# Two units ahead of the FFN's norm, norm factors with positions on partitions, shorter routing, unread products in waits, and plain loads of the down tiles

## Chip, cores and metric

The kernel runs on one core of one Trainium2 chip. The metric is the time of one execution in device microseconds (us). A trace of one profiled execution tells what each engine did; its times count from the first instruction of the span.

## What is computed

A trunk of two layers over one sequence of 256 positions with 1024 features, all in float32. Each layer has a mixer and a channel mixer (FFN), each behind an RMS norm that is shifted and scaled by a conditioning vector. The FFN of layer 0 is dense; that of layer 1 sends each position to 2 of 8 experts.

```python
for l in range(DEPTH):
    mod = cond @ w_ada[l] + b_ada[l]
    sh_m, sc_m, gt_m, sh_f, sc_f, gt_f = jnp.split(mod[:, None, :], 6, axis=-1)
    h = _rmsnorm(x, g_norm_mix[l]) * (1 + sc_m) + sh_m
    x = x + gt_m * _hybrid_mixer(h, ...)
    h = _rmsnorm(x, g_norm_ffn[l]) * (1 + sc_f) + sh_f
    y = _swiglu(h, ...) if l % 2 == 0 else _moe(h, ...)     # d_ff 2816
    x = x + gt_f * y
return _rmsnorm(x, g_final)
# _swiglu: (silu(h @ w_gate) * (h @ w_up)) @ w_down
# _moe: logits = h @ w_router + b_router; top 2 of 8; softmax over the two; sum of gate_e * _swiglu_e(h)
```

## The kernel before, in words

**Data.** x is kept as xT, eight tiles k of 128 features by 256 positions. Weights come from HBM through SP's DMA queue, as "units" of at most 1 MB each (256 columns or 256 rows of a matrix), in the order in which they are used, into a ring of buffers; a unit is loaded as soon as a buffer is free (`fill`). Outside the experts a product of two float32 matrices is made as three fp32r products (L654 to L656): each operand is cut into a high part (a cast, ScalarE, "hi") and a rest (a subtraction, VectorE, "lo") by `split`, 1.9 and 2.2 us for a unit of 1024 x 256. A unit of 256 output columns then takes 8 k x 2 x 3 = 48 products of 256 columns. Units without a key are those of the ada matrix (`ada_unit`); VectorE alone works on them, and `ada_tail` or `ada_wide` turn their sums into columns of M.

**Stages.** Mixer 0 (to about 163 us), dense FFN (to about 358), mixer 1 (to about 495), experts (to about 1203), final norm. `row_product` makes the last product of a mixer or FFN, adds it into xT tile by tile (two j at a time) and, in `done`, squares each new tile for the sums of the norm that follows.

**Norms** (`rms_mod`, L772). While the last xT tiles are finished, `scaled_parts` cuts A*xT, not yet normalised, into "xa" (high and rest). The first unit of the next stage is multiplied with xa: L792 to L794, 48 products into two PSUM banks. Between them stand, at k = SUMK = 2, the last sums of squares over partitions (L861) and a copy of the sums ("rows"), and at k = ACROSS = 4 a product with ones (L786) that puts the sum on all partitions, 128x256; `nrstd` turns it into the factor rs_ (square root on ScalarE, reciprocal and one Newton step on VectorE, all 128x256). Then the eight tiles are normalised (ht) and cut (hh on ScalarE, hl on VectorE), and the next unit can be multiplied (`feat_major`, L654 to L656). `start(c, dst)` multiplies the products made ahead by rs_ and returns a bias. In the dense FFN the unit made ahead is ("gate", 0) and the first behind the norm ("up", 0); in mixer 1 it is ("xl", 1, 0).

**End of mixer 1.** `route_sums` takes for each j two products with the router's matrix (L1227), two transposes of xT into PSUM banks "ps_xt" (L1229) and, through `sums_small`, products of the squares with ones (L301). `ada_wide` makes the columns of ada group (1, 5), wanted only at the kernel's end: eight products (L416), a copy, a transpose (L418), an addition into M.

**Routing** (`moe`, from L1232). y is the norm's factor for each position, lg the logits, sel the two chosen experts of each position. Products L1268 to L1272 (bank "ps_pos") count places; posp is the place of a position in its expert's list, and `oh` the one-hot matrix of it. `normalised` makes xnh and xnl (high part and rest of the normalised rows with positions on partitions) from the transposes. `gather(0)` multiplies them with oh (L1443) into xf, the 96 rows of expert place 0; later gathers do so for the other sets.

**Experts.** Eight places, each of the kind M (CAP 96 rows) or S (64 rows): KINDS = "MSMMSMMS". Each goes over d_ff in groups of 1024, 1024 and 768 columns: four gate tiles and four up tiles (L1462 for S, L1469 for M, plain fp32), then `act` and, one group later, `turn` (transposes of the activations, L1499, L1502 and L1385) and `down` (L1539 for M, L1557 for S). The weights stay whole (`whole`), and each buffer is free when PE has used it. For kind M the last group of 768 rows of the down matrix is laid out so that two tiles are strided reads of 128 partitions, and the third consists of two transfers of 512 KB to 64 partitions each (L325, the list path of `load`).

**Order.** An automatic scheduler orders the instructions on each engine; ScalarE's and VectorE's instructions behind a `hold()` are not put ahead of it. `limit` and state["limit"] say up to which unit splits may run ahead; `next_unit` does the next one.

## Time and profile before

| | us |
|---|---|
| three runs, median | 1223.89 |
| lowest and highest | 1220.61, 1226.54 |
| the profiled execution's own time | 1221.15 |
| its span, first to last instruction | 1219.4 |
| PE busy | 1158.0 |
| VectorE busy | 517.6 |
| ScalarE busy | 308.2 |
| mean granted clock of PE (1 is full) | 0.981 |

In the rows, PE is TensorE's products and PEld its weight loads, DVE is VectorE, ACT ScalarE, SP the engine that issues the loads. A name like "ps_z<-hh,hi" says what is written and what is read. A timeline row gives start, duration, engine, line, operation, the count of merged instructions, and in brackets how long the engine was idle before and what released it. L112 is the line of a helper through which all ScalarE and VectorE instructions pass. Instructions on PE overlap: the time from one start to the next is shorter than the duration.

### The profile page before, as it was taken

To read this page: it belongs to the slowest core of one execution; us is meant where nothing else is said; L and a number is where in the kernel's file an instruction comes from. 1 tells how busy PE (TensorE), PEld (TensorE's weight loads), DVE (VectorE), ACT (ScalarE), POOL (GpSimd) and SP (SyncE) were. 2 spreads that over 40 slices of the span, in tenths; PEclk is the share of its full clock that TensorE was granted. 3 is DMA by queue.
4 is the path that set the end of the run, shared out by engine and by line. 5 is a ranking of instruction groups with operands and counts; after the bars stand their busy time and mean duration, and the time that the engine had idled before them with its cause. 6 is when DMAs were issued, how large, how long until landed. Compare 5 with 4: busy or idle time off the path is not lost.

```text
span 1219.4 us, 28948 instructions
## 1 busy us (share of the span) xinstructions
PE 1158.0 (95%) x12777; PEld 853.2 (70%) x12777; DVE 517.6 (42%) x947; ACT 308.2 (25%) x528; POOL 18.2 (1%) x49
## 2 busy tenths in 40 slices
PE   3899989999998999899999999999999999999994
PEld 3798879999997998666644667767545576666531
DVE  6799989988768985410110111020010111010123
ACT  3493465344346834200100001000000000000111
POOL 4000000000010000000000000000000000000000
PEclk9899999999999999799999999999999999999998
DMA  9976739989862856889999999999999999999991
GB/s 321 351 263 221 273 142 360 356 318 345 281 213 72 281 179 245 342 300 405 357 412 416 411 408 377 370 404 369 379 409 414 413 410 325 403 400 334 404 396 63
DMA packets 144419, 400.66 MB, mean 329 GB/s; under 512 B 6968, under 2 KB 50288, under 8 KB 144288
## 3 DMA queue, kind: packets, MB, share of 16 engines
q1 hardware_dynamic: 143296, 397.44, 87.5%
q8 instruction: 102, 1.67, 0.5%
q0 software_dynamic: 560, 1.16, 0.4%
q10 hardware_dynamic: 432, 0.15, 0.1%
q14 instruction: 29, 0.24, 0.1%
HBM read 397.67 MB, written 1.05 MB: 327 GB/s over the span
## 4 chain that ended last, share of the span: by engine, by line
PE 87%; DVE 8%; ACT 2%; issue 1%; DMA 1%; ACTq 0%; SPq 0%; DVEq 0%
PE ps_y L1539 12%; PE ps_g L1469 8%; PE ps_u L1469 8%; PE ps_gu L1469 8%; PE ps_z L656 5%; PE ps_z L654 5%; PE ps_z L655 5%; PE ps_g L1462 5%; PE ps_u L1462 5%; PE ps_y L1557 5%; PE ps_acc L654 2%; PE ps_acc L656 2%; PE ps_acc L655 2%; PE ps_acc L829 2%; PE ps_xg L1443 2%; DVE lo L112 2%
## 5 line engine op out<-in xcount | busy, mean ns | idle before, releaser
L654 PE MATMUL ps_z<-hh,hi 128*128 128x256 f32 x624 | 177.3, 285 | 4.6 <-ACT hh L112 3.9
L656 PE MATMUL ps_z<-hh,lo 128*128 128x256 f32 x624 | 175.8, 284 | 2.0 <-DVE lo L112 2.0
L655 PE MATMUL ps_z<-hl,hi 128*128 128x256 f32 x624 | 176.7, 284 | 0.1
L1469 PE MATMUL ps_gu<-raw,xf 128*32 128x256 f32 (+1 forms) x1920 | 151.1, 365 | 2.9 <-issue 2.9
L1539 PE MATMUL ps_y<-raw,aT 128*32 128x256 f32 (+1 forms) x1980 | 150.0, 451 | 0.0
L112 DVE TENSOR_TENSOR lo<-raw,hi 128x2048 fp32r<-128x2048 f32 x60 | 136.5, 2284 | 17.7 <-ACT sg L112 9.2
L1539 PEld LDWEIGHTS ps_y<-raw,aT 128*32 128x32 f32 x1980 | 93.0, 110 | 51.4 <-issue 2.4
L112 ACT CAST hi<-raw 128x2048 fp32r<-128x2048 f32 x59 | 111.8, 1905 | 56.5 <-PE ps_acc L655 26.5
L1469 PE MATMUL ps_g<-raw,xf 128*32 128x256 f32 (+1 forms) x1920 | 125.5, 367 | 0.0
L654 PEld LDWEIGHTS ps_z<-hh,hi 128*128 128x128 f32 x624 | 119.4, 192 | 5.7 <-ACT hh L112 4.1
L112 DVE SCALAR_TENSOR_TENSOR a<-a,gs,ps_u 128x256 f32<-128x256 f32 (+3 forms) x39 | 18.7, 512 | 246.3 <-PE ps_u L1469 118.9
L1469 PE MATMUL ps_u<-raw,xf 128*32 128x256 f32 (+1 forms) x1920 | 121.1, 364 | 0.2 <-issue 0.2
L656 PEld LDWEIGHTS ps_z<-hh,lo 128*128 128x128 f32 x624 | 118.6, 191 | 2.3 <-DVE lo L112 2.3
L655 PEld LDWEIGHTS ps_z<-hl,hi 128*128 128x128 f32 x624 | 119.5, 192 | 0.4 <-DVE hl L112 0.3
L112 DVE SCALAR_TENSOR_TENSOR acc<-raw,cond,acc 128x1024 f32<-128x1024 f32 x77 | 98.4, 1278 | 4.1 <-DMA raw<-in_w_ada_dram 3.2
L1469 PEld LDWEIGHTS ps_gu<-raw,xf 128*32 128x32 f32 x1920 | 71.1, 111 | 32.2 <-issue 4.9
L1469 PEld LDWEIGHTS ps_g<-raw,xf 128*32 128x32 f32 x1920 | 66.9, 111 | 33.3 <-issue 6.8
L1469 PEld LDWEIGHTS ps_u<-raw,xf 128*32 128x32 f32 x1920 | 68.6, 111 | 28.0 <-issue 2.4
L112 ACT COPY aT<-ps_t 128x512 f32<-128x512 f32 (+1 forms) x24 | 13.2, 550 | 257.6 <-PE ps_t L1514 164.5
L112 DVE COPY aT<-ps_t 128x256 f32<-128x256 f32 (+1 forms) x20 | 7.8, 390 | 143.2 <-PE ps_t L1514 73.1
L1462 PE MATMUL ps_g<-raw,xf 128*64 128x512 f32 (+1 forms) x288 | 61.8, 563 | 0.0
L1462 PE MATMUL ps_u<-raw,xf 128*64 128x512 f32 (+1 forms) x288 | 59.6, 559 | 0.0
(485 smaller groups left out, 1498.7 us busy)
## 6 DMA issues: line engine op xcount, KB each, us to landing
raw<-in_w_exp_down_dram SPq DMA_DIRECT2D x83, 1024.0 KB, 17.5
raw<-in_w_exp_gate_dram SPq DMA_DIRECT2D x64, 1024.0 KB, 17.6
raw<-in_w_exp_up_dram SPq DMA_DIRECT2D x64, 1024.0 KB, 17.9
raw<-in_w_ada_dram SPq DMA_DIRECT2D x40, 1024.0 KB, 5.8
raw<-in_w_in_dram SPq DMA_DIRECT2D x24, 1024.0 KB, 6.6
raw<-in_w_exp_gate_dram SPq DMA_DIRECT2D x32, 768.0 KB, 16.4
raw<-in_w_exp_up_dram SPq DMA_DIRECT2D x32, 768.0 KB, 14.8
raw<-in_w_ff_gate_dram SPq DMA_DIRECT2D x11, 1024.0 KB, 7.5
```

What stands on the lines that cost most here:

```text
L112: r = op(*a, **kw)
L654: TE.matmul(ps, wh, xh, start=first, stop=False, **kw)
L655: TE.matmul(ps, wh, xl, start=False, stop=False, **kw)
L656: TE.matmul(ps, wl, xh, start=False, stop=last, **kw)
L829: TE.matmul(out_, w[:, c, js], parts[c], start=start, stop=stop, skip_group_check=True)
L1443: TE.matmul(p, src[:, t, k * P:(k + 1) * P], oh[:, t, :w], start=n == 0 and t == 0, stop=n == 1 and t == 1)
L1462: TE.matmul(ps[0][b * 64:b * 64 + 64, :h], xf[:, k, :], w[:, q, b * h:(b + 1) * h], start=k == 0, stop=k == KD - 1)
L1469: TE.matmul(o[j * 32:j * 32 + 32], xf[:, k, g * 32:g * 32 + 32], w[:, q, j * h:(j + 1) * h], start=k == 0 and (g == 0 or g == 2 and key == ...
L1539: TE.matmul(y[bank_][r:r + 32, c:c + nd], x(g), w[:, b, d0:d0 + nd], start=first and start, stop=last, skip_group_check=True)
L1557: TE.matmul(y[0][h2 * 64:h2 * 64 + 64], ah[:, o + b * 64:o + b * 64 + 64], w[:, c, ns], start=first, stop=last)
```

## The change

1. `rms_mod` takes a list of units. The dense FFN multiplies gate 0 and up 0 with xa ahead of the norm; mixer 1 still one unit. The sums stand at step 2, the factor at step 4, its spread over the partitions at step 7, counted over both units. The factor is made with positions on partitions (128x2): two products with a column of ones, `nrstd` on 128x2, then `all_across` (two diagonal matrices, two fp32 products) and a ScalarE copy to rs_. The next unit's split (gate 1) stands ahead of the normalisation.
2. `route_sums` no longer uses sums of squares by products; ScalarE squares the transposed banks with a running sum (four instructions of 128x512), and `done` makes no squares there.
3. `ada_wide` is cut in two: the eight products and the bias stay, copy, transpose and addition move to expert 0.
4. In `moe`, four ScalarE copies make the normalised rows xn (float32); the first gather uses xn and oh as fp32; xnh and xnl are made in expert 0's second group.
5. `warm(n)` issues n products of 128x512 (fp32r, ones by ones) that nobody reads: 12 behind the ada products, 3 behind the place products, 6 behind mixer 1's products ahead of the norm.
6. The last down tiles of kind M are plain loads of 256 rows; `turn` makes the matching layout with three banks and three more transposes, `down` picks its columns accordingly.
7. ss0 and nw0, at the kernel's beginning, lie in another pool.

```diff
+WARM = 12, 3, 6
+SUMS_AT, FACTOR_AT, ACROSS_AT = 2, 4, 7
...
     def load(ap, shape, pool=rawp, tag="raw"):
-        if isinstance(ap, list):
-            v = raw[:, :shape[0] * shape[1]].rearrange("p (a b) -> p a b", a=shape[0])
-            for i, x in enumerate(ap):
-                nc.sync.dma_start(v[i * 64:(i + 1) * 64], x)
-            return v
...
     def ada_wide(l, g):
+        acc, ps = accs.pop((l, g)), bank("ps_ada")
         for j in range(KD):
             TE.matmul(ps[:KD, :P], pick[:, j, :], acc[:, j * P:(j + 1) * P], start=j == 0, stop=j == KD - 1)
-        S.copy(am, ps[:KD, :P])
-        TE.transpose(ps[:, P:P + KD], am, ident[:KD, :KD])
-        V.tensor_add(M[l][:, g * KD:(g + 1) * KD], ps[:, P:P + KD], colr("b_ada", l * 48 + g * KD, KD, C1))
-        known.add((l, g))
+        m = M[l][:, g * KD:(g + 1) * KD]
+        V.tensor_copy(m, colr("b_ada", l * 48 + g * KD, KD, C1))
+
+        def turned(pool):
+            am = pool.tile([P, P], F32, name="am")[:KD]
+            S.copy(am, ps[:KD, :P])
+            TE.transpose(ps[:, P:P + KD], am, ident[:KD, :KD])
+            V.tensor_add(m, ps[:, P:P + KD], m)
+            known.add((l, g))
+        late.append(turned)
+
+    def warm(n):
+        ps = bank("ps_warm")
+        for i in range(n):
+            TE.matmul(ps.rearrange("p (a b) -> p a b", a=4), onesr, onesr[:, None, :].to_broadcast([P, 4, P]),
+                      start=True, stop=True)
...
                         w = expert("w_exp_down", t)[r0:r0 + n, :]
-                        if KINDS[t] == "M" and n == 768:
-                            if m < 2:
-                                return w.rearrange("(j r) f -> r j f", j=4)[:P, 2 * m:2 * m + 2]
-                            w = w.rearrange("(a b r) f -> b r a f", a=2, b=2)
-                            return [w[b, P:] for b in range(2)]
                         return w[m * 256:(m + 1) * 256].rearrange("(k p) f -> p k f", p=P)
...
-    def rms_mod(pool, key):
+    def rms_mod(pool, keys):
...
-            if k == ACROSS:
-                ps = bank("ps_rs")
-                TE.matmul(ps[:, :T], ones, rows, start=True, stop=True)
-                rs_ = nrstd([pool.tile([P, T], F32, name="rs_", tag="hn", bufs=2)] + ..., ps[:, :T], 1.0 / (32 * D), T)
+        for u, key in enumerate(keys):
+            hi, lo = take(key)
+            for k in range(KD):
+                at = u * KD + k
...
+                if at == FACTOR_AT:
+                    ps = bank("ps_n")
+                    for t in range(2):
+                        TE.matmul(ps[:, t:t + 1], rows[:, t * P:(t + 1) * P], ones[:, 0:1], start=t == 0, stop=True,
+                                  skip_group_check=True)
+                    y = nrstd(small.tile([P, 6], F32, name="nwx", tag="nwx"), ps[:, 0:2], 1.0 / (32 * D), 2)
+                if at == ACROSS_AT:
+                    psr = all_across(y)
+                    rs_ = pool.tile([P, T], F32, name="rs_", tag="hn", bufs=2)
+                    S.copy(rs_, psr)
...
+        if len(keys) == 1:
+            warm(WARM[2])
+        state["limit"] = next(i for i in range(state["take"], len(units)) if units[i]["key"]) + 1
+        next_unit()
         hh, hl, ht = norm_tiles(pool)
...
-        hh, hl, start = rms_mod(fp, ("gate", 0))
+        hh, hl, start = rms_mod(fp, (("gate", 0), ("up", 0)))
...
+                    su = fp.tile([P, T], F32, name="su", tag="su", bufs=2)
+                    V.scalar_tensor_tensor(sg, su, start(1, c, su), sg, op0=ALU.add, op1=ALU.mult)
...
-        sums_small(st, j, KD, sq, False)
+        if j % 4 == 3:
+            for t in range(2):
+                junk = pre.tile([P, D], F32, name="rj", tag="acc", bufs=2)[:, :512]
+                S.activation(junk, rt["x", j // 4][t], AF.Square, accum_out=rt["sq"][:, j // 4, t:t + 1])
...
-        y = nrstd(small.tile([P, 6], F32, name="nwr"), rt["st"][:, 0:2], 1.0 / D, 2)
+        V.tensor_add(rt["sq"][:, 0, :], rt["sq"][:, 0, :], rt["sq"][:, 1, :])
+        y = nrstd(small.tile([P, 6], F32, name="nwr", tag="nwx"), rt["sq"][:, 0, :], 1.0 / D, 2)
+        xn = yacc
+        for q in range(2):
+            for t in range(2):
+                S.activation(xn[:, t, q * 512:(q + 1) * 512], rt["x", q][t], AF.Copy, scale=y[:, t:t + 1])
...
-        normalised(0, 0)
+        warm(WARM[1])
+
+        def in_parts():
+            for t in range(2):
+                S.copy(xnh[:, t, :], xn[:, t, :])
+                V.tensor_sub(xnl[:, t, :], xn[:, t, :], xnh[:, t, :].bitcast(F32))
...
-                for t, q in ((1, 0), (0, 1), (1, 1)):
-                    normalised(t, q)
-                hold()
...
-                for n, src in enumerate((xnh, xnl)):
+                srcs = (xn,) if es[0] == 0 else (xnh, xnl)
+                for n, src in enumerate(srcs):
                     for t in range(2):
+                        o = oh[:, t, :w]
+                        TE.matmul(p, src[:, t, k * P:(k + 1) * P], o.bitcast(F32) if es[0] == 0 else o,
+                                  start=n == 0 and t == 0, stop=n == len(srcs) - 1 and t == 1)
...
             if kd == "M" and n == 768:
-                p1, p2 = bank("ps_t"), bank("ps_t")
-                for g in range(3):
-                    TE.transpose(p1[:, g * P:(g + 1) * P], a[:, g * 192:g * 192 + P], ident)
+                p0, p1, p2 = (bank("ps_t") for _ in range(3))
                 for g in range(3):
-                    c, x = slice(g * P, (g + 1) * P), a[:, g * 192 + P:(g + 1) * 192]
-                    TE.transpose(p2[:64, c], x, ident)
-                    turned_to(p2[64:, c], x)
+                    c, x = slice(g * P, (g + 1) * P), a[:, g * 192:(g + 1) * 192]
+                    TE.transpose(p0[:, c], x[:, :P], ident)
+                    TE.transpose(p1[:, c], x[:, 64:], ident)
+                    TE.transpose(p2[:64, c], x[:, P:], ident)
+                    turned_to(p2[64:, c], x[:, :64])
...
                 if e == 0 and i == 0:
                     shares()
                     arrange()
+                    late.pop()(ep)
                 if e == 0 and i == 1:
                     places()
+                    in_parts()
```

## Rows read from the trace of the kernel before

**Rows 1.** The page, part 1 (busy us, share, instructions) and part 4 (chain)

```profile
PE 1158.0 (95%) x12777; PEld 853.2 (70%) x12777; DVE 517.6 (42%) x947; ACT 308.2 (25%) x528; POOL 18.2 (1%) x49
...
PE 87%; DVE 8%; ACT 2%; issue 1%; DMA 1%; ACTq 0%; SPq 0%; DVEq 0%
```

**Rows 2.** PE's waits, 515 to 1203 us: us in total, times, longest

```profile
PE ps_gu L1469 <- issue: 2.9, 2, 2.5
```

**Rows 3.** Windows: PE, PEld, DVE, ACT, POOL busy (instructions), PEclk, DMA share, GB/s

```profile
515.00:1203.00 688.00, 682.02 (x9215) 411.32 (x9207) 83.99 (x190) 48.19 (x95) 0.60 (x1) 1.00 1.00 379
1022.00:1040.00 18.00, 16.13 (x297) 10.31 (x289) 0.87 (x3) 1.07 (x2) 0.00 (x0) 1.00 1.03 246
1038.00:1044.00 6.00, 3.53 (x37) 1.95 (x36) 0.00 (x0) 0.00 (x0) 0.00 (x0) 0.72 1.00 401
```

**Rows 4.** DMA issues: count, KB each, median us from issue to landing

```profile
raw<-in_w_exp_down_dram SPq DMA_DIRECT2D x83, 1024.0 KB, 17.5
...
raw<-in_w_exp_down_dram SPq DMA_DIRECT2D x10, 512.0 KB, 20.8
```

**Rows 5.** Timeline of SP's DMA queue, the last weight issues: start, us, operation

```profile
1164.66 14.63 SPq L333 DMA_DIRECT2D raw<-in_w_exp_down_dram  x7
```

**Rows 6.** Timeline of PE, the last down products

```profile
1199.49 3.65 PE L1557 MATMUL ps_y<-raw,aT 128*64 128x512 f32 x16
```

**Rows 7.** Timeline around the FFN's norm: start, us, engine, line [idle before <-releaser]

```profile
167.35 0.59 PE L786 MATMUL ps_rs<-rows,ones 128*128 128x256 f32 x2
...
167.98 0.47 ACT L112 ACTIVATE nu<-ps_rs,epsc 128x256 f32<-128x256 f32 x1 [0.86 <-PE ps_rs L786]
...
168.49 0.42 DVE L112 TENSOR_SCALAR nh<-ps_rs 128x256 f32<-128x256 f32 x1 [4.38 <-ACT nu L112]
...
168.83 1.74 DVE L112 RECIPROCAL rs__1769<-nu 128x256 f32<-128x256 f32 x1
...
173.07 0.51 PE L654 MATMUL ps_z<-hh,hi 128*128 128x256 f32 x2 [3.93 <-ACT hh L112]
```

**Rows 8.** Window behind the FFN's norm, columns as in rows 3

```profile
173.10:177.40 4.30, 4.17 (x20) 3.95 (x21) 4.30 (x12) 2.17 (x6) 0.00 (x0) 0.60 0.02 4
```

**Rows 9.** Window over 512-column fp32r products of mixer 0, columns as in rows 3

```profile
53.19:57.40 4.21, 4.21 (x19) 3.38 (x18) 4.21 (x20) 0.00 (x0) 0.00 (x0) 1.00 1.08 404
```

**Rows 10.** Timeline of DVE behind the FFN's norm: two splits

```profile
180.06 4.49 DVE L112 TENSOR_TENSOR lo<-raw,hi 128x2048 fp32r<-128x2048 f32 x2
```

**Rows 11.** Timeline of PE at mixer 1's norm

```profile
373.31 0.36 PE L900 MATMUL ps_gt<-hh,wgh 128*128 128x256 f32 x1 [3.55 <-ACT hh L112]
```

**Rows 12.** Window in mixer 1 behind its norm, columns as in rows 3

```profile
380.00:410.00 30.00, 26.58 (x164) 23.23 (x163) 29.14 (x46) 26.27 (x40) 0.00 (x0) 1.00 0.68 230
```

**Rows 13.** Timeline from mixer 1's end to the first expert

```profile
493.12 0.51 PE L301 MATMUL ps_st<-ones,sqs 128*128 128x1 f32 x4
...
496.61 0.26 ACT L112 ACTIVATE nwr<-ps_st,epsc 128x2 f32<-128x2 f32 x1 [3.56 <-PE ps_st L301]
...
498.64 0.17 DVE L112 TENSOR_TENSOR M<-ps_ada,C 128x8 f32<-128x8 f32 x1 [0.92 <-PE ps_ada L418]
498.64 2.42 ACT L112 ACTIVATE xnh<-ps_xt,nwr 128x512 fp32r<-128x512 f32 x4 [0.32 <-PE ps_ada L418]
...
500.84 0.27 PE L1268 MATMUL ps_pos<-sel,before 128*128 128x8 f32 x1 [2.24 <-DVE sel L112]
...
502.36 0.63 PE L1443 MATMUL ps_xg<-oh,xnh 128*128 128x96 f32 x2 [0.66 <-DVE oh L112]
...
515.07 0.81 PE L1469 MATMUL ps_g<-raw,xf 128*32 128x256 f32 x9
```

**Rows 14.** Windows, place products to first expert, columns as in rows 3

```profile
501.50:515.00 13.50, 12.84 (x79) 9.45 (x83) 8.85 (x45) 4.40 (x7) 0.00 (x0) 0.50 0.82 325
515.00:520.20 5.20, 5.20 (x100) 2.88 (x96) 0.00 (x0) 0.00 (x0) 0.00 (x0) 1.00 0.71 221
```

**Rows 15.** Timeline of PE, transposes ahead of a large expert's last down group

```profile
765.76 0.55 PE L1499 MATMUL ps_t<-ident,a 128*128 128x128 f32 x3
```

More of the change, by code (lines that the diff above doesn't have):

```diff
@@ L799, in rms_mod, with start @@
         hold()
-        def start(c, dst):
+        def start(u, c, dst):
             bias = pre.tile([P, 1], F32, name="bz", tag="bz", bufs=2)
-            V.tensor_mul(dst, res[c][:, :T], rs_)
-            V.tensor_reduce(bias, res[c][:, T:T + 2], axis=AX.X, op=ALU.add)
+            V.tensor_mul(dst, res[u][c][:, :T], rs_)
+            V.tensor_reduce(bias, res[u][c][:, T:T + 2], axis=AX.X, op=ALU.add)
             return bias
@@ L1214, in route_setup @@
         TE.matmul(ps[:, :NE], ones, wsum, start=True, stop=True)
+        rt["sq"] = small.tile([P, 2, 2], F32, name="rsq")
         cr = rt["cr"] = small.tile([P, NE], F32, name="cr")
```

77 lines of the change are left out of this document (36 added, 41 removed).

## The prediction

> **What bounds the kernel now.** I read four views. First the page: TensorE (PE) is busy 1158.0 of 1219.4 us, and the chain that ended last is 87% PE and 8% VectorE (DVE) [rows 1]. So a part of the change counts only by what it does to PE's idle time, to PE's clock, or to the products PE must run. Second, PE's waits in the expert stage: from 515 to 1203 us PE is idle 6 us, and the longest group of waits is 2.9 us for "issue", that is, for nothing the trace shows; no wait for a weight transfer is in that list [rows 2, 3]. The reader should set this against the DMA share of 1.00 in the same stretch [rows 3]: the transfer engines are always busy and PE still never waits for them, because weights are loaded far ahead. How far: the last seven down tiles are issued until 1164.66 + 14.63 = 1179.3, one lands 17.5 us after its issue in the median [rows 4, 5], so the last lands near 1196.8; PE starts its last two tiles (16 instructions over 3.65 us) at 1199.49 [rows 6], so the last tile's turn comes near 1201.3. That lead of some 4 to 5 us is about the smallest, and it sets what DMA savings can be worth. Third, the timelines of three places where PE does wait or loses clock: the FFN's norm, the norm of mixer 1, and the routing. Fourth, windows over the same places for the granted clock.
>
> The profiled execution took 1221.15 us (span 1219.4); the sum is made against it. The median of the runs shown is 2.7 us more.
>
> **FFN norm, two units ahead.** Now PE has 48 products on the unnormalised input and then stands idle 3.93 us until 173.07 [rows 7]; after that it runs 4.30 us at clock 0.60 [rows 8], which costs 4.30 x 0.40 = 1.7 us. Together 5.6 us. The change puts up 0's 48 products into that wait. A product with 512 columns takes 4.21 / 18 = 0.23 us [rows 9] (of the 19 in that row one began before), so one with 256 takes about 0.117, and 48 take 5.6: more than the idle time. The products are moved from behind the norm, not added, so the whole idle time can go. The factor's chain must be over by then. Before: square root 167.98, a reciprocal of 1.74 on 128x256, then three operations of about 0.42, about 172.0 [rows 7]. After: the square root and the Newton steps work on 128x2; such a chain took from 496.61 to 498.64 - 0.92 = 497.72, so 1.1 us [rows 13], then two small DVE operations (at most 0.42 each), two fp32 products (at most 0.59 each) and a copy (at most 0.47) [rows 7]: ready by 171.6 at the latest, nearer 170.8. PE gets its first normalised tile 173.07 - 172.0 = 1.1 us later, at about 172, and PE is busy with up 0 until 169.14 + 5.6 = 174.7. Cover: 2 to 3 us.
> What eats it: the split of gate 1 now stands ahead of the normalisation, 2.24 us of DVE (4.49 for two) [rows 10] and a cast on ScalarE. DVE was idle 4.38 us before 168.49 [rows 7], and nothing in the split needs the norm, so I take it to fall in that gap at no cost; if it runs behind the factor, normalisation starts near 174, PE waits up to 1.5 us, and the splits of the next two units come late, 2 to 3.5 us in all. What is late next is DVE: from 173.1 to 177.4 it is busy all 4.30 us [rows 8]. I give back 0.6 for that: **-5.0** (ends -2.0 and -6.0; the lower end adds 0.4 for a unit that no longer waits for its split).
>
> **Mixer 1's norm.** Same chain, one unit only. PE is idle 3.55 us before 373.31 [rows 11]. The new chain is 0.4 to 1.6 us shorter, and six unread products (6 x 0.23 = 1.4 us) fall into the wait and cost nothing while it is longer than that; 3.55 - 1.6 = 1.95 still is. They may keep the clock up behind it. But from 380 to 410 DVE is busy 29.14 of 30 us and PE 26.58 [rows 12]: part of what PE gains there it loses again to DVE. **-1.5** (-0.5 to -3.0).
>
> **Routing to the first expert.** (a) Eight groups of column sums (L301) go from PE's queue, 0.51 us each as recorded [rows 13]; a record's tail lies under the next product, so I count 0.37 each: 3.0 us of PE work that stood ahead of or between the last transposes, 2.6 of it before the last of them. In its place ScalarE squares four 128x512 banks; the two that come last are on the path, at 0.6 each (four passes over such banks in 2.42) [rows 13], and one small add. Net: factor ready 1.4 + 0.6 (the last sum's wait) = 2.0 us earlier. (b) The bias add of ada (1,5) goes from DVE's path: DVE stood 0.92 us before it and it stands between the factor and the logits [rows 13]: -1.0. So the selection and PE's place products come 3.0 earlier. PE waits 2.24 us for the selection now [rows 13]. In that wait come 12 unread products, 12 x 0.23 = 2.8 us. PE's end before the wait also moves 3.0 forward, so they overlap the wait and might outlast it by 0.5. Gather products would start near 502.36 - 3.0 + 0.2 = 499.5. (c) From 501.5 to 515 PE runs at clock 0.50, the lower of its two levels (1.2 of 2.4 GHz), for 13.5 us [rows 14], the largest single loss in the trace. With the clock at full, and with 16 fp32 products of 96 columns instead of 32 (0.22 each at most, by proportion from 0.59 for 256 columns [rows 7], tail included; I take 0.19) the gather needs 3.0 us. The first gate tile, 48 instructions, needs 2.5: at full clock behind 515, 100 instructions took 5.20 [rows 14]. ScalarE's and DVE's shifts of the gathered rows may add 0.6. The second gate tile starts near 499.5 + 3.0 + 2.5 + 0.6 = 505.6, against 515.07 [rows 13]: **-9.5** (ends -4.0, clock not held, and -11.0). The later split of the gathered source (two casts, two subtractions on engines that are busy 84 and 48 of 688 us [rows 3]) and the bias add in the first expert cost nothing while they are hidden there; uncovered, about 0.3 for the ada transpose on PE.
> The Trainium skill ("TensorE: Matmul & The Clock Gate", Part 4, PE-mode transpose) says that a transpose does not count as PE work for the clock in the way a product does. By it the clock could fall earlier here, since the stretch ahead of the wait is mostly transposes; that is the first rival below. The rows don't settle it: the low clock begins behind a wait of 2.24 us [rows 13, 14].
>
> **Down tiles as plain loads.** In each of five large experts, the last down group was read by two strided transfers and two of 512 KB to 64 partitions (10 in all, 20.8 us to landing) [rows 4]. The traffic falls then: 246 GB/s from 1022 to 1040 against 379 over the stage [rows 3]. There are five such dips; this is one of the longest. Over the stage PE is not waiting for a transfer, so a faster one gives nothing directly.
> The Trainium skill ("DMA: Bandwidth & Descriptors", Rules for kernel authors) says of two transfers to disjoint halves of the partitions: use one over 128 partitions instead. The rows agree that traffic falls at these tiles; whether that is worth anything is decided by PE's waits, and by these it is not.
> What may go is PE's "issue" wait of 2.5 us just as that dip ends, with clock 0.72 over the 6 us around it [rows 2, 3]: 2.5 + 6 x 0.28 = 4.2. If its cause is code that arrives late because transfers are slow, it goes: -4.2; if not, 0; I take -3.0 for the coincidence in time. The price is certain: three more 128-column transposes in each of five experts; three such transposes were recorded at 0.55 with the tail, so about 0.4 [rows 15], and 5 x 0.4 = 2.0: **+2.0**.
> A coupling: PE enters the expert stage about 16 us earlier, of which 6.5 shift everything ahead as well, and the routing's 9.5 shorten the lead of the weights by as much, less what the DMA engines did not use there (share 0.82 over 13.5 us, so 2.4 us [rows 14]). A lead of 4 to 5 us could not bear that; the dips' removal gives it back (18 x (1 - 246/379) = 6.3 us in one dip alone).
>
> **Sum.** -5.0 - 1.5 - 9.5 - 3.0 + 2.0 = -17.0: 1221.15 - 17.0 = 1204.2. Towards the median of runs I add 1: **1205**.
>
> **Rivals.**
> 1. The clock isn't held at the routing: the unread products depend on nothing there, so they can be put into earlier gaps, ahead of the real wait, or they run at half clock and delay the place products by 12 x 0.47 - 2.24 = 3.4 us. The routing then gives -3 instead of -9.5: about 1211. For it: PE has small gaps before; against it: they stand behind the last ada products in the program. 0.18.
> 2. DVE becomes the bound behind the FFN's norm, because gate 1's split runs ahead of the normalisation: that part gives -2: about 1208. For it: DVE full at 173 to 177 [rows 8]. 0.13.
> 3. The transfers bound the expert stage after all, since their share is 1.00: then five dips of about 5 to 6 us return up to 28 us: 1204 - 14 = about 1190. Against: no wait for a weight [rows 2]. 0.04.
> 4. The change does not do what it says for the traffic: the dips have another cause and stay. The issue wait stays, and the shortened lead makes PE wait 3 us: 1204 + 3 + 3 = 1210. 0.10.
> 5. Slower: code. If more instruction fetches come late in the expert stage (each 4.2 us with its clock loss), the gain of 17 is gone at four of them, and six give 1204 + 25 = about 1229. For it: PE waited for "issue" there twice [rows 2]; against it: only one was long. 0.04.
> The forecast itself has 0.51.
>
> **Chances and range.** About 0.5% (6.1 us) is what a measurement here can tell from no change. Forecast and rivals 1 to 4 lie below 1217.8 but for two of them together: faster 0.89, same 0.07, slower 0.04. Range: best ends 1221.15 - 6 - 3 - 11 - 4.2 + 2 = 1199, worst ends 1221.15 - 2 - 0.5 - 4 + 0 + 2 = 1216.7; with 2 us of scatter below, 1197 to 1217.
>
> **What would show it.** FFN norm right: PE's wait for the first normalised tile under 1 us and full clock behind it; wrong: a wait for hh or lo of 2 us or more. Routing right: granted clock 1.00 from 490 on and the second gate tile near 500 (505.6 less the 6.5 saved before); wrong: clock 0.50 behind the place products. Down tiles right: no 512 KB transfers, no stretch near 246 GB/s, no issue wait over 2 us, and transposes 2 us dearer. The forecast is wrong if the gain in the expert stage itself, first gate tile to last product, is over 6 us (rival 3) or negative by over 3 (rivals 4, 5).

## The result, and the profile after

The changed kernel takes 1208.53 us in the median (1208.46 to 1211.94, four runs), the kernel before 1222.39 us (four runs); the ratio is 0.9897, with a 95% interval of 0.9875 to 0.9919. In a second set of runs the changed kernel had 1209.27 us and 0.9901 (0.9880 to 0.9922). So it is about 1% faster, 13.9 us by the medians, where 18.9 had been forecast from median to median. The profiled execution of the changed kernel took 1208.46 us, with a span of 1206.7.

The page's parts 1 and 4 for the changed kernel, beside [rows 1]:

```profile
PE 1153.8 (96%) x12793; PEld 849.7 (70%) x12793; DVE 514.6 (43%) x955; ACT 310.7 (26%) x537; POOL 18.2 (2%) x49
...
PE 87%; DVE 8%; DMA 2%; ACT 1%; issue 1%; ACTq 0%; DVEq 0%
```

PE is still the bound. To see where the time went, I cut each trace at the same five starts on PE: the first product on the unnormalised input in the FFN, the first in mixer 1, the last product of the high part `mah` with a high part in mixer 1 (0.24 us ahead of its very last), the second gate tile of the first expert, and the first product of the final combination. "Front" is the time ahead of the first of these, which the change touches only in the place of two small tiles (item 7). Stages in us, worked out from these starts:

| kernel traced | front | dense FFN | mixer 1 | routing | experts | span |
|---|---|---|---|---|---|---|
| before | 158.32 | 201.37 | 131.48 | 23.90 | 689.50 | 1219.44 |
| before, second trace | 160.83 | 201.39 | 131.49 | 23.89 | 685.16 | 1217.59 |
| changed | 158.80 | 198.13 | 128.16 | 16.80 | 689.70 | 1206.67 |
| changed, second trace | 158.88 | 198.14 | 128.15 | 16.81 | 687.70 | 1204.76 |

The three stages in the middle repeat within 0.02 us, so a difference of a few tenths there is one of the program. The front and the experts do not: they move by 2.5 and 4.3 us between two traces of the same kernel. Between the first traces the gain is 3.2 in the FFN, 3.3 in mixer 1 and 7.1 in the routing; the experts gained nothing.

**FFN norm.** Timeline of the changed kernel around the FFN's norm (start, us, engine, line, operation), beside [rows 7] and [rows 10]:

```profile
168.38 0.26 ACT L117 ACTIVATE nwx<-ps_n,epsc 128x2 f32<-128x2 f32 x1 [0.77 <-PE ps_n L799]
168.54 1.89 ACT L117 CAST hi<-raw 128x2048 fp32r<-128x2048 f32 x1
...
169.53 0.48 DVE L117 TENSOR_SCALAR dg<-ident,nwx 128x128 f32<-128x128 f32 x2
...
170.46 2.29 DVE L117 TENSOR_TENSOR lo<-raw,hi 128x2048 fp32r<-128x2048 f32 x1 [0.46 <-ACT hi L117]
...
176.10 0.28 PE L662 MATMUL ps_z<-hh,hi 128*128 128x256 f32 x1
...
183.81 0.51 PE L664 MATMUL ps_z<-hh,lo 128*128 128x256 f32 x2 [1.34 <-DVE lo L117]
190.56 0.39 PE L663 MATMUL ps_acc<-al,hi 128*128 128x256 f32 x1 [0.82 <-DVE al L117]
```

The square root and the Newton step are on 128x2; from the square root to the diagonal matrices the chain takes 1.6 us. At 176.10 PE goes from the unnormalised to the normalised input with no wait, where it stood 3.93 us before. But the split of gate 1 stands at 170.46, between the factor and the normalisation, and at 183.81 and 190.56 PE waits for VectorE. Windows there (PE, PEld, DVE, ACT, POOL busy, PEclk, DMA share, GB/s):

```profile
180.00:184.00 4.00, 2.66 (x22) 2.47 (x22) 4.00 (x6) 4.00 (x3) 0.00 (x0) 1.00 0.29 68
188.00:192.00 4.00, 3.17 (x27) 2.97 (x27) 4.00 (x4) 1.37 (x4) 0.00 (x0) 1.00 0.93 305
```

VectorE is busy 4.00 of 4.00 us in both, PE 2.66 and 3.17: VectorE has become the bound for some us.

**Mixer 1's norm.** Timeline of PE in the changed kernel, beside [rows 11]:

```profile
367.53 1.52 PE L433 MATMUL ps_warm<-onesr 128*128 128x512 f32 x6
...
369.08 0.35 PE L921 MATMUL ps_gt<-hh,wgh 128*128 128x256 f32 x1
```

The unread products take the place of the wait; the first normalised product follows them directly. Counted from the stage's start it comes at 12.15 us instead of 13.62. Windows behind it, kernel before, then the changed one:

```profile
375.00:378.40 3.40, 3.40 (x18) 3.40 (x17) 3.22 (x9) 2.30 (x6) 0.00 (x0) 0.50 0.02 5
369.00:375.00 6.00, 5.98 (x48) 5.78 (x48) 5.82 (x17) 3.87 (x8) 0.00 (x0) 1.00 0.01 3
```

Before, the clock was 0.50 in this stretch, shortly behind the wait of 3.55 us, which cost 1.7 us (3.4 x 0.50); now it stays at 1.00. A later wait for ScalarE grew from 1.15 to 2.56 us and took most of that back:

```profile
384.01 0.31 PE L956 MATMUL ps_gz<-ident,g 40*128 40x40 f32 x2 [1.15 <-ACT g L112]
379.78 0.31 PE L977 MATMUL ps_gz<-ident,g 40*128 40x40 f32 x2 [2.56 <-ACT g L117]
```

**Routing.** Timeline of the changed kernel, beside [rows 13], and windows over the same stretch, beside [rows 14] (a plain fp32 product shows as two instructions):

```profile
490.25 3.06 PE L433 MATMUL ps_warm<-onesr 128*128 128x512 f32 x12
...
493.67 0.27 PE L1304 MATMUL ps_pos<-sel,before 128*128 128x8 f32 x1 [0.36 <-DVE sel L117]
...
494.25 0.94 PE L433 MATMUL ps_warm<-onesr 128*128 128x512 f32 x3
...
495.05 3.34 PE L1478 MATMUL ps_xg<-oh,yacc 128*128 128x96 f32 x28
...
498.32 1.07 PE L1504 MATMUL ps_g<-raw,xf 128*32 128x256 f32 x16
```

```profile
490.00:495.05 5.05, 4.69 (x23) 3.28 (x22) 3.47 (x18) 3.88 (x9) 0.00 (x0) 1.00 1.03 411
495.05:498.30 3.25, 3.25 (x29) 3.17 (x28) 3.03 (x12) 2.54 (x5) 0.00 (x0) 1.00 1.02 405
498.30:501.90 3.60, 3.60 (x55) 2.11 (x57) 3.04 (x18) 2.82 (x5) 0.00 (x0) 1.00 1.03 411
```

The wait for the selection is 0.36 us instead of 2.24, the granted clock is 1.00 throughout instead of 0.50, and the gather plus the first gate tile take 6.84 us (495.05 to the second tile at 501.89) instead of 12.71.

**Experts.** Windows of the changed kernel over the stage and over the stretch that answers to the dip of [rows 3], and the issues of the down tiles, beside [rows 4]:

```profile
503.00:1190.00 687.00, 681.91 (x9211) 412.07 (x9203) 85.74 (x199) 48.95 (x100) 0.60 (x1) 1.00 0.98 383
1009.00:1027.00 18.00, 18.00 (x277) 11.52 (x274) 0.72 (x2) 0.63 (x2) 0.00 (x0) 1.00 1.02 407
```

```profile
raw<-in_w_exp_down_dram SPq DMA_DIRECT2D x88, 1024.0 KB, 11.4
```

The dip is gone (407 GB/s instead of 246), and a down tile lands 11.4 us after its issue instead of 17.5. The stage takes PE the same time: the transposes are added, and it still loses to waits for "issue", now elsewhere.

```profile
831.64 0.53 PE L1504 MATMUL ps_u<-raw,xf 128*32 128x192 f32 x8 [0.89 <-issue]
838.13 0.53 PE L1504 MATMUL ps_gu<-raw,xf 128*32 128x192 f32 x8 [1.08 <-issue]
```

### The profile page after: what moved, and what is told of

Same layout as the page of the kernel before. It is cut to its first block, busy times and chain, and to the rows that moved or that the text cites. A ratio compares the mean times of both kernels' runs of the same rounds, so it can differ in the third digit from the quotient of the medians.

```text
span 1206.7 us, 28978 instructions
## 1 busy us (share of the span) xinstructions
PE 1153.8 (96%) x12793; PEld 849.7 (70%) x12793; DVE 514.6 (43%) x955; ACT 310.7 (26%) x537; POOL 18.2 (2%) x49
## 4 chain that ended last, share of the span: by engine, by line
PE 87%; DVE 8%; DMA 2%; ACT 1%; issue 1%; ACTq 0%; DVEq 0%
PE ps_y L1579 12%; PE ps_g L1504 8%; PE ps_u L1504 8%; PE ps_gu L1504 8%; PE ps_y L1597 5%; PE ps_g L1497 5%; PE ps_u L1497 5%; PE ps_z L664 5%; PE ps_z L662 5%; PE ps_z L663 5%; PE ps_acc L662 2%; PE ps_acc L664 2%; PE ps_acc L663 2%; PE ps_acc L850 2%; DVE lo L117 2%
## 5 line engine op out<-in xcount | busy, mean ns | idle before, releaser
L664 PE MATMUL ps_z<-hh,lo 128*128 128x256 f32 x608 | 170.5, 282 | 3.3 <-DVE lo L117 3.3
L662 PE MATMUL ps_z<-hh,hi 128*128 128x256 f32 x608 | 171.8, 283 | 0.2 <-ACT hi L117 0.2
L663 PE MATMUL ps_z<-hl,hi 128*128 128x256 f32 x608 | 170.7, 281 | 0.0
L1504 PE MATMUL ps_g<-raw,xf 128*32 128x256 f32 (+1 forms) x1920 | 122.5, 362 | 0.0
L664 PEld LDWEIGHTS ps_z<-hh,lo 128*128 128x128 f32 x608 | 114.5, 189 | 3.8 <-DVE lo L117 3.8
L662 PEld LDWEIGHTS ps_z<-hh,hi 128*128 128x128 f32 x608 | 115.4, 190 | 0.9 <-ACT hi L117 0.6
L663 PEld LDWEIGHTS ps_z<-hl,hi 128*128 128x128 f32 x608 | 115.0, 189 | 0.1
L117 ACT COPY aT<-ps_t 128x512 f32<-128x512 f32 (+3 forms) x29 | 14.0, 481 | 266.3 <-PE ps_t L1554 177.7
L117 DVE COPY aT<-ps_t 128x256 f32<-128x256 f32 (+2 forms) x20 | 7.8, 392 | 145.3 <-PE ps_t L1554 73.1
L1597 PE MATMUL ps_y<-raw,aT 128*64 128x512 f32 x264 | 60.2, 608 | 0.6 <-ACT aT L117 0.6
## 6 DMA issues: line engine op xcount, KB each, us to landing
raw<-in_w_exp_down_dram SPq DMA_DIRECT2D x88, 1024.0 KB, 11.4
```

Source lines behind the costliest of these rows:

```text
L117: r = op(*a, **kw)
L662: TE.matmul(ps, wh, xh, start=first, stop=False, **kw)
L663: TE.matmul(ps, wh, xl, start=False, stop=False, **kw)
L664: TE.matmul(ps, wl, xh, start=False, stop=last, **kw)
L1504: TE.matmul(o[j * 32:j * 32 + 32], xf[:, k, g * 32:g * 32 + 32], w[:, q, j * h:(j + 1) * h], start=k == 0 and (g == 0 or g == 2 and key == ...
L1597: TE.matmul(y[0][h2 * 64:h2 * 64 + 64], ah[:, o + b * 64:o + b * 64 + 64], w[:, c, ns], start=first, stop=last)
```

## Experiments

In each, the time is the median of its runs and the ratio is to the kernel before on the same chip. For small effects the stage of the trace decides, since the front and the experts scatter by more than the effects. All traces, stages as above:

| kernel traced | dense FFN | mixer 1 | routing | experts |
|---|---|---|---|---|
| before, two traces | 201.37, 201.39 | 131.48, 131.49 | 23.90, 23.89 | 689.50, 685.16 |
| changed, two traces | 198.13, 198.14 | 128.16, 128.15 | 16.80, 16.81 | 689.70, 687.70 |
| one unit ahead | 199.93 | 128.25 | 16.81 | 687.47 |
| early split | 200.99 | 128.35 | 16.80 | 686.54 |
| early split, own low tile | 197.68 | 128.18 | 16.80 | 689.84 |
| the same, spread later | 198.96 | 128.34 | 16.80 | 685.64 |
| no unread products | 198.13 | 128.34 | 19.65 | 688.60 |
| fewer unread products | 198.14 | 128.37 | 16.80 | 690.50 |
| fp32r gather | 198.14 | 128.35 | 22.21 | 687.44 |
| fp32r gather, waits filled | 198.13 | 128.37 | 22.15 | 691.69 |
| old down tiles | 198.14 | 128.34 | 16.80 | 696.65 |
| before with new down tiles | 201.39 | 131.48 | 23.84 | 687.48 |

### The FFN: one unit ahead

```diff
-        hh, hl, start = rms_mod(fp, (("gate", 0), ("up", 0)))
+        hh, hl, start = rms_mod(fp, (("gate", 0),))
```

(The second unit is then made behind the norm, as in the kernel before.)

> The changed kernel with one edit: the dense FFN multiplies only gate 0 ahead of its norm, as the kernel before did; the shorter factor chain and all else stay. Theory 1 (PE's wait for the norm decides; two units cover it): between the last product on the unnormalised input and the first normalised tile PE waits again, 3.93 us less the 1 to 1.6 us by which the new factor chain is shorter, and the clock falls behind it for about 1.7 us: 2 to 4 us slower than the changed kernel, 1210.5 to 1212.5. Rival (VectorE decides: its splits and normalisation set when the later units can run, whatever stands ahead): under 1 us slower, 1208.5 to 1209.5.

1211.03 us (ratio 0.9916, 0.9887 to 0.9945); dense stage 199.93, 1.80 us over the changed kernel. Timeline at the norm and the window behind it:

```profile
172.81 1.27 DVE L117 SCALAR_TENSOR_TENSOR ht<-xT,A,rs__1802 128x256 f32<-128x256 f32 x3 [1.01 <-ACT rs__1802 L117]
...
173.89 0.50 PE L662 MATMUL ps_z<-hh,hi 128*128 128x256 f32 x2 [1.52 <-ACT hh L117]
```

```profile
173.90:178.00 4.10, 3.96 (x19) 3.75 (x20) 4.10 (x12) 2.04 (x5) 0.00 (x0) 0.62 0.02 4
```

So the wait and the low clock (0.62) are back. The wait is 1.52 us, 2.4 less than before. VectorE starts the normalisation (ht) 12.22 us after the stage's start, 1.45 earlier than in the kernel before. Of the FFN's gain of 3.24 us, 1.44 is thus the shorter factor chain and 1.80 the second unit. That is just under what theory 1 asked for, and well under the 3.1 us that the wait and the clock (4.10 x 0.38) add up to: against the rest stand the changed kernel's two waits for VectorE (1.34 and 0.82 us), which this one does not have there.

### The FFN: the split of gate 1 earlier, three steps

```diff
+        taken = [take(key) for key in keys]
+        hold()
+        state["limit"] = next(i for i in range(state["take"], len(units)) if units[i]["key"]) + 1
+        next_unit()
+        hold()
...
-        state["limit"] = next(i for i in range(state["take"], len(units)) if units[i]["key"]) + 1
-        next_unit()
         hh, hl, ht = norm_tiles(pool)
```

> The changed kernel with one edit: gate 1's split is put behind the last pieces of the unnormalised input and ahead of the sums, on ScalarE and VectorE, where both were idle for about 4 us, instead of between the factor and the normalisation. Theory 1 (the part of the FFN gain that was missing was lost because VectorE was late by that split): the normalisation starts about 1.7 us earlier, PE's wait for a split of 1.3 us and the one of 0.8 us behind it go: 1.5 to 2.5 us faster than the changed kernel, 1206.0 to 1207.0. Rival (VectorE's ada sums behind the normalisation make it late, or the buffers of the splits): 0 to 0.5 us faster, 1208.0 to 1208.5.

1213.11 us (0.9928, 0.9899 to 0.9956); dense stage 200.99, 2.86 slower than the changed kernel, which neither theory had. VectorE's timeline:

```profile
170.86 2.29 DVE L117 TENSOR_TENSOR lo<-raw,hi 128x2048 fp32r<-128x2048 f32 x1 [4.67 <-PE ps_z L815]
```

The split stood where I wanted it and waited 4.67 us for a buffer: the three low buffers hold the unnormalised input, gate 0 and up 0, and the first is free when PE has finished gate 0. The factor, behind it on VectorE, waited too; PE waited 3.15 us for the diagonal matrices and ran at half clock behind that wait. In the changed kernel the same three buffers are in use, so there too the split could not have run in VectorE's idle time.

```diff
-        lo = splp.tile([P, 2048], F32R, tag="lo", name="lo", bufs=3)
+        if u["key"] == ("gate", 1):
+            lo = state["own"].tile([P, 2048], F32R, name="lo1")
+        else:
+            lo = splp.tile([P, 2048], F32R, tag="lo", name="lo", bufs=3)
```

> The early split of gate 1 with one more edit: its low part goes to a tile of its own, since in the run before VectorE waited 4.67 us for PE to finish gate 0 (the three low buffers held the unnormalised input, gate 0 and up 0). Theory 1 (the buffer alone stood in the way, and VectorE's lateness by this split is what was missing of the FFN gain): the split runs in VectorE's idle time before the factor, normalisation starts 1.7 us earlier than in the changed kernel, the dense stage (first product on the unnormalised input to mixer 1's) falls from 198.1 to 195.7 to 196.7 us. Rival (the ada sums behind the normalisation keep VectorE late): 197.6 to 198.2 us.

1210.32 us (0.9894, 0.9872 to 0.9916); dense stage 197.68, 0.46 faster than the changed kernel, in the rival's range. The split now ran at 168.61, in the idle time, but PE reached the spread of the factor too early and waited 1.53 us there for the diagonal matrices:

```profile
168.61 2.29 DVE L117 TENSOR_TENSOR lo<-raw,hi 128x2048 fp32r<-128x2048 f32 x1 [1.31 <-ACT hi L117]
...
173.75 0.71 PE L287 MATMUL ps_rs<-dg,ones 128*128 128x128 f32 x4 [1.53 <-DVE dg L117]
...
174.90 1.28 DVE L117 SCALAR_TENSOR_TENSOR ht<-xT,A,rs__1808 128x256 f32<-128x256 f32 x3 [1.01 <-ACT rs__1808 L117]
```

The third step moved the spread:

```diff
-                if at == ACROSS_AT:
+                if at == (9 if len(keys) == 2 else ACROSS_AT):
```

> The early split with a low tile of its own, and the spread of the factor over the partitions two steps later in PE's order (step 9 instead of 7 in the FFN only). In the run before PE waited 1.5 us for the diagonal matrices there, with products left that could have run. Theory 1 (that wait took back what the early split gave): the dense stage falls by 1.0 to 1.6 us more, from 197.7 to 196.1 to 196.7 us, and the kernel is about 2 us faster than the changed kernel. Rival (VectorE's ada sums behind the normalisation set the pace): 197.4 to 197.7 us, and waits for the low parts come back.

1210.56 us (0.9921, 0.9903 to 0.9940); dense stage 198.96, slower than both. Timeline at and behind the norm:

```profile
174.77 1.28 DVE L117 SCALAR_TENSOR_TENSOR ht<-xT,A,rs__1822 128x256 f32<-128x256 f32 x3 [2.31 <-ACT rs__1822 L117]
...
185.93 0.51 PE L667 MATMUL ps_z<-hh,lo 128*128 128x256 f32 x2 [2.39 <-DVE lo L117]
192.67 0.39 PE L666 MATMUL ps_acc<-al,hi 128*128 128x256 f32 x1 [0.82 <-DVE al L117]
```

Theory 1 falls. The rival stands in kind, though the stage is 1.3 us slower than it said: what PE no longer waits for at the spread it waits for at the next split (2.39 us instead of 1.34). The three kernels with two units ahead and full clock show what sets the time. VectorE begins the normalisation (ht) at 174.90 (own low tile), 172.67 (changed kernel) and 174.77 (spread later); counted from the stage's start (161.51, 158.80 and 160.08) that is 13.40, 13.87 and 14.69 us, and the stage ends 184.3 us after it in all three. So the time follows the start of the normalisation one for one; PE's waits only change place. Which of VectorE's steps behind it (normalisation, ada sums, splits) would have to move was not tried.

### The unread products

```diff
-WARM = 12, 3, 6
+WARM = 0, 0, 0
```

> The changed kernel without any of the 21 unread products. Theory 1 (they hold the clock): PE idles about 3 us before the place products and runs at clock 0.50 behind them, so gather and first gate tiles cost about twice for some us, and in mixer 1 the clock falls behind the norm: 4 to 7 us slower, 1212.5 to 1215.5. Rival (the shorter waits alone keep the clock): 0 to 0.5 us faster than the changed kernel, 1208.0 to 1208.5, with the granted clock at 1.00 from the place products on.

1212.87 us (0.9928, 0.9901 to 0.9955). Routing 19.65, 2.85 slower; mixer 1 128.34. Windows of the routing:

```profile
492.30:495.90 3.60, 0.25 (x4) 0.00 (x1) 2.88 (x14) 2.43 (x6) 0.00 (x0) 1.00 1.02 410
495.90:503.40 7.50, 7.13 (x36) 6.92 (x36) 3.25 (x14) 4.19 (x8) 0.00 (x0) 0.54 1.03 409
```

PE is idle 3.35 of 3.60 us ahead of the place products and then runs 7.5 us at 0.54. Theory 1 holds for the routing, but with 2.9 us instead of 4 to 7. In mixer 1 it does not: PE waits 1.38 us for the first normalised product (at 371.12), and the clock behind it stays at 1.00.

```profile
371.00:377.00 6.00, 5.88 (x47) 5.73 (x47) 5.82 (x17) 3.87 (x8) 0.00 (x0) 1.00 0.01 3
```

The stage is 0.19 us longer than in the changed kernel, but five other kernels that keep the six products have 128.34 to 128.37 too, so they are worth nothing that can be told.

```diff
-WARM = 12, 3, 6
+WARM = 6, 3, 0
```

> The changed kernel with 6 unread products instead of 12 behind the ada products, 3 behind the place products as before, none in mixer 1. Theory 1 (what counts is that PE's wait for the selection is short enough): PE waits about 1.7 us for the selection, the clock may fall as in the run without any; routing stage (last mixer product to second gate tile) 16.8 us if the clock stays at 1.00, 18.5 to 19.7 if it falls to 0.50; mixer 1 within 0.2 us of the changed kernel's 128.16. Rival (mixer 1 needs its six): mixer 1 over 128.6 us.

1210.09 us (0.9904, 0.9881 to 0.9926); routing 16.80, as with twelve, at clock 1.00, although PE waits 1.75 us for the selection:

```profile
495.37 0.27 PE L1306 MATMUL ps_pos<-sel,before 128*128 128x8 f32 x1 [1.75 <-DVE sel L117]
```

```profile
496.70:504.00 7.30, 7.30 (x87) 5.56 (x90) 6.52 (x31) 5.42 (x9) 0.00 (x0) 1.00 1.03 409
```

Half of them do the same, and mixer 1 (128.37) does not need its six.

### The first gather

```diff
-                srcs = (xn,) if es[0] == 0 else (xnh, xnl)
+                srcs = (xnh, xnl)
...
-                        TE.matmul(p, src[:, t, k * P:(k + 1) * P], o.bitcast(F32) if es[0] == 0 else o,
+                        TE.matmul(p, src[:, t, k * P:(k + 1) * P], o,
```

(The parts are made ahead of the gather instead of in the first expert.)

> The changed kernel with the first gather as the kernel before made it: 32 fp32r products on the high and low parts, both made ahead of it, instead of 16 fp32 products on the rows themselves. Theory 1 (the clock and the shorter chain made the gain; the products themselves cost the same, 32 x 0.105 at full clock against 16 x 0.21): the products cost 0 to 0.3 us more, but the two subtractions of 1.22 us stand ahead of the second half: routing stage 17.3 to 19.3 us instead of 16.8. Rival (the plain fp32 gather is a large part of the gain of 7 us in that stage): 20 us or more.

1213.85 us (0.9945, 0.9930 to 0.9961); routing 22.21, 5.4 slower. The rival holds. Windows over the gather and the first gate tile:

```profile
496.60:504.60 8.00, 7.21 (x34) 6.73 (x33) 6.75 (x35) 5.22 (x9) 0.00 (x0) 0.57 1.02 408
504.60:508.90 4.30, 4.30 (x53) 2.08 (x56) 1.84 (x8) 0.00 (x0) 0.00 (x0) 0.61 1.03 408
```

The clock falls to 0.50 within the gather, in spite of all the unread products. The lost clock (8.0 x 0.43 + 4.3 x 0.39 = 5.1 us) is nearly all of the 5.4. Two short waits stand in the gather, 0.29 and 0.50 us. The last run fills them:

```diff
-WARM = 12, 3, 6
+WARM = 12, 9, 6
```

> The kernel of the run before with the fp32r gather, and nine unread products behind the place products instead of three, so that PE's two short waits inside the gather (0.29 us for the high part, 0.50 us for the low part) are filled: 6 x 0.23 = 1.4 us more. Theory 1 (the two waits let the clock fall there): granted clock 1.00 through the gather, 32 products at about 0.105 each, routing stage about 18 to 19 us. Rival (the gather of 128x96 fp32r products itself does not hold the clock, waits or not): 0.50 within or behind the gather again, routing stage 21 us or more.

One run, 1218.05 us beside 1223.95 of the kernel before. Routing 22.15, as the rival had it. Windows:

```profile
496.50:502.60 6.10, 5.74 (x38) 4.98 (x37) 5.77 (x30) 4.39 (x8) 0.00 (x0) 0.98 1.03 409
502.60:509.00 6.40, 6.40 (x48) 3.32 (x51) 2.82 (x13) 1.72 (x2) 0.00 (x0) 0.50 1.02 408
```

Nearly all of the gather runs at full clock this time, but then the clock is 0.50 for 6.4 us. So in these two traces the clock falls whether the two waits are there or not; with 16 fp32 products in the gather's place it stays. Why is not shown. Other small gaps of 0.1 to 0.2 us remained in the gather, and the kind of product alone does not do it: the three later gathers of every kernel are of this kind too (32 fp32r products of 160 or 256 columns), and from their first to their last product the clock was 1.00 in 39 of the 42 cases in these traces. One of them, in the trace with the fp32r first gather:

```profile
577.00:584.00 7.00, 6.27 (x46) 4.51 (x48) 2.78 (x7) 2.27 (x5) 0.00 (x0) 1.00 1.03 408
```

### The down tiles

The changed kernel with the old layout (list path in `load`, strided tiles, nine transposes):

```diff
-                        return w[m * 256:(m + 1) * 256].rearrange("(k p) f -> p k f", p=P)
+                        if KINDS[t] == "M" and n == 768:
+                            if m < 2:
+                                return w.rearrange("(j r) f -> r j f", j=4)[:P, 2 * m:2 * m + 2]
+                            w = w.rearrange("(a b r) f -> b r a f", a=2, b=2)
+                            return [w[b, P:] for b in range(2)]
+                        return w[m * 256:(m + 1) * 256].rearrange("(k p) f -> p k f", p=P)
```

> The changed kernel with the old down tiles (strided loads, two 64-partition transfers in each large expert, nine transposes instead of twelve). Theory 1 (PE bounds the expert stage and the loads are hidden): PE saves 5 x 0.4 = 2 us of transposes and the dips of the traffic stay hidden: 1206.5. Rival 1 (the shorter routing used up the lead of the weights, which was about 6 us at its least before): PE waits for weights 2 to 4 us: 1208.5 to 1210.5, with waits for a DMA in PE's list. Rival 2 (slow transfers make code late): waits for issue of over 4 us in all come back: 1208.5 to 1211.

1215.93 us (0.9958, 0.9939 to 0.9978). Experts 696.65: 7 to 9 us slower than the two traces of the changed kernel. The ratios say the same: 0.9958 against 0.9897 and 0.9901 is 7.0 to 7.5 us. PE's waits of the whole span that name a transfer of the experts' weights (us in total, times, longest):

```profile
PE ps_y L1603 <- DMA raw<-in_w_exp_down_dram: 3.8, 7, 0.6
...
PE ps_u L1515 <- DMA raw<-in_w_exp_gate_dram: 1.8, 1, 1.8
...
PE ps_g L1515 <- DMA raw<-in_w_exp_gate_dram: 1.1, 2, 0.7
...
PE ps_u L1508 <- DMA raw<-in_w_exp_up_dram: 1.1, 3, 0.5
```

Together 7.8 us, where neither the kernel before nor the changed one has any in this stage. Some 4 us of it stand between 919 and 1042 us, the rest at the last tiles, from 1170 us on. Rival 1 holds, at twice the size I gave it; that the shorter routing did it rather than the shorter stages before it was not separated.

The kernel before with the new layout alone:

> The kernel before with one edit: the new down tiles (plain loads, twelve transposes). Theory 1 (PE bounds the expert stage, the dips are hidden as long as the lead of the weights lasts): from the second gate tile to the last down product the stage changes by +2.0 us of transposes, and waits for issue change by chance: -2.5 to +2 against the kernel before, 1219 to 1225. Rival (the transfers bound the stage also there): 5 us or more faster than before.

1220.81 us, ratio 0.9993 (0.9977 to 1.0009): nothing that can be measured. Experts 687.48, between the two traces of the kernel before. Alone the new tiles are worth nothing; in the changed kernel, with its shorter stages ahead of the experts, they are worth 7 to 9 us.

### Second traces

> The changed kernel unchanged, for a second trace and as a measure on the same chip. Theory 1: the stages ahead of the experts repeat within 0.3 us, the time ahead of the dense stage and the waits for issue in the expert stage differ by 1 to 3 us from run to run. Rival: the waits for issue stand in the same places with the same lengths, so they belong to the program.

1209.27 us (0.9901, 0.9880 to 0.9922). The stages ahead of the experts are the same; the waits for issue are shorter (0.54 near 837, where it had 0.89 and 1.08) and the experts 2.0 us faster.

> The kernel before unchanged, for a second trace. Theory 1 (the 2.5 us wait for issue near 1038 us comes from the slow transfers at that place): it is there again. Rival (chance): it is gone or elsewhere.

PE's timeline in the second trace of the kernel before:

```profile
1039.67 0.64 PE L1469 MATMUL ps_gu<-raw,xf 128*32 128x256 f32 x8 [1.15 <-issue]
1047.53 1.07 PE L1469 MATMUL ps_u<-raw,xf 128*32 128x256 f32 x16 [0.74 <-issue]
```

The wait at that dip is there again, before the same product, but at 1.15 us instead of 2.47, and the clock stays at full from 1038 to 1044 instead of 0.72. So its place repeats and its size does not. The experts took 4.3 us less than in the first trace. Windows, the first trace twice, then the second over most of the stage:

```profile
1009.00:1014.00 5.00, 4.76 (x22) 2.56 (x23) 1.14 (x3) 0.97 (x2) 0.06 (x1) 0.66 1.03 416
1040.00:1045.00 5.00, 4.40 (x52) 2.66 (x55) 0.00 (x0) 0.00 (x0) 0.00 (x0) 0.66 1.03 418
515.00:1185.00 670.00, 666.48 (x9174) 406.69 (x9168) 84.08 (x192) 47.78 (x94) 0.60 (x1) 1.00 1.01 384
```

The first trace has two stretches at half clock, each of which costs 1.7 us (5.0 x 0.34); the second has none. The prediction knew one of them. With about 1 us less of waits for issue, that is the 4.3 us.

## Why the prediction was right or wrong

The forecast was 1205 us, and the time of 1208.53 lies in the range of 1197 to 1217. Step by step, from the first traces:

| term | forecast | measured |
|---|---|---|
| FFN norm | -5.0 (-2.0 to -6.0) | -3.2 |
| mixer 1's norm | -1.5 (-0.5 to -3.0) | -1.8 |
| routing | -9.5 (-4.0 to -11.0) | -8.6 |
| issue wait | -3.0 (0 to -4.2) | not separable |
| transposes | +2.0 | +1.9 |
| experts, both together | -1.0 | +0.2 (first traces) |

(The transposes are worked out from the time between the two weight tiles around them, 0.38 to 0.39 us more in each of the five large experts. Mixer 1's stage fell by 3.32; four of the eight groups of sums at 0.37 us, 1.5 us, lay ahead of its last product and belong to the routing's term, as the prediction counted it.)

**FFN.** The step that failed is "I take it to fall in that gap at no cost", with "I give back 0.6 for that". The split ran behind the factor: it started when its cast on ScalarE was done, and put earlier it waited for a low buffer. So VectorE began the normalisation 13.87 us after the stage's start, where the kernel with one unit, which has no split there, began at 12.22. Those 1.65 us are the whole shortfall of 1.8 but for 0.1, since the stage follows that start one for one; begun at 12.22, by that rule (an estimate, no run), it would have gained 4.9. PE's waits show it as 1.34 + 0.82 us against the 0.6 given back. The cover itself was right: no wait at 176.10. Rival 2 described what happened, at a smaller price (it gave -2.0). What the prediction did not see is that moving the split does not help as it stands: three attempts put the dense stage between 197.68 and 200.99.

**Mixer 1.** Right in size, and the parts add up: the first normalised product 1.5 us earlier, 1.7 of lost clock gone, 1.4 lost again, at a wait for ScalarE rather than VectorE. The prediction had not entered the lost clock. It said that the unread products may keep the clock up; they are not the reason, since without them it stays at 1.00 too. What changed is the wait ahead of it, 1.38 us without them instead of 3.55.

**Routing.** Right in size and in its parts: counted from mixer 1's start and less the 1.8 us of its norm, the gather starts 2.7 us earlier, forecast 2.9; from there to the second gate tile it is 6.84 us, forecast 6.1. But the prediction put the held clock down to the unread products, so its number is in part luck. They are worth 2.85 us; the fp32 gather, which the prediction had entered only for its count of products, is worth 5.4, nearly all of it clock, because with the other gather the clock falls in spite of them. The first rival, the clock not held, came true in those experiments (19.65 and 22.2 us) and not in the changed kernel. The prediction also called the stretch ahead of the wait mostly transposes; in the trace of the kernel before, between mixer 1's last product and that wait, 9 of PE's 57 instructions are transposes.

**Down tiles.** That faster transfers give nothing directly was right: the kernel before with the new tiles alone is at 0.9993. The coupling was right in kind and too small in size. I wrote that the lead of 4 to 5 us could not bear the shorter routing, and gave 3 us for the case that the dips stay (rival 4); the old tiles in the changed kernel cost 7 to 9. The lead was taken from the last tile alone, and about half of the waits stand earlier. Rival 3, up to 28 us from the transfers, is excluded.
The step "-3.0" for the issue wait failed. I took a coincidence in time for a price; a second trace of the kernel before has the wait at less than half and no loss of clock. With the new tiles the changed kernel does not have that wait, and others of 0.5 to 1.1 us stand elsewhere. In the ten traces of the changed kernel and its variants with the new tiles the stage lies between 685.6 and 691.7 us. The forecast's -1.0 and the measured +0.2 are both inside that scatter.

**The sum.** FFN +1.8, routing +0.9, experts +1.2, front +0.5 and mixer 1 -0.3 make up, with 0.2 at the kernel's end and but for rounding, the 4.2 us between the forecast of -17.0 and the spans' -12.8. No version tried is measurably faster than the changed kernel; the early split with its own low tile has the shortest dense stage and no better time.

## What to carry to other kernels

When a shorter chain lets the bound engine start a long stage earlier, price the lead of its loads at the place where it is least: loads that were hidden become the bound, and a change of the loads that is worth nothing alone may be what keeps the gain. When a wait on one engine is filled with work, look at which engine made that wait and what else it has to do behind it; buffers, not only idle time, say whether a step can move. A wait for which a profile names no cause should have its size taken from several traces before it is entered in a sum.

## What the runs showed that was not expected

- The clock fell with the fp32r first gather (32 products of 128x96) and stayed with 16 fp32 ones, with the same 15 unread products ahead of it: 0.57 and 0.61 in two windows against 1.00; six more unread products in the place of the two waits moved the fall to the gather's end and left the stage at 22.15 us. Later fp32r gathers mostly kept the clock, so the cause stays open. The Trainium skill ("TensorE: Matmul & The Clock Gate", Part 4, PE-mode transpose) sets transposes apart from products in what they do for the clock; no run here isolates transposes.
- Without unread products an idle time of 3.35 us was followed by half clock; with six of them a wait of 1.75 us was not.
- The front, the same code in all these kernels but for the place of two small tiles, took between 158.3 and 162.5 us, and the experts moved by 2.0 and 4.3 us between two traces of one kernel, while the stages between repeated within 0.02 us. The spread of the runs comes from these two ends.
- In the expert stage PE ran at half clock for some us in ten of the fourteen traces, at a cost of 1.7 to 5.1 us in all, and not at the same places. With the waits for issue this makes most of the stage's scatter.
